# Order of the products, the forget rows, the early up pairs and the last statistics of a decoder layer on one core

## The chip, the core and the metric

The kernel runs on one core of a Trainium2 chip. The metric is the device time of one execution in microseconds (us), the median of the runs. Below, PE is TensorE (PEld its weight loads), DVE is VectorE, ACT is ScalarE, POOL is GpSimd and SP is SyncE, which issues the DMAs.

## The reference

One decoder layer on 1024 positions of width 1024, in fp32. What matters here:

```python
# z = h @ W_in: gates, queries, keys, values and the forget rows of the recurrence
f = lb + (1.0 - lb) * jax.nn.sigmoid(f_logit)
log_f = jnp.log(f); k = 1.0 - f
b = jnp.cumsum(gc, axis=3)               # gc: log_f in chunks of 64 positions
q_in = qc * jnp.exp(b); k_in = kc * jnp.exp(-b); k_out = kc * jnp.exp(b_last - b)
# three mixers: the recurrence, window attention, attention into a memory; gated sum; then
h = layer_norm(alpha * h + mix, g1, b1)
h = layer_norm(alpha * h + relu(h @ W_up)**2 @ W_down, g2, b2)
```

## The kernel before

**Products.** Every 32-bit factor is split into a high and a low part (`split`, lines 76 and 77: ACT casts the high part, then DVE or POOL subtracts to get the low one). The large products are done two row blocks at a time, a *pair*, with seven smaller products in place of eight, numbered 1 to 7 in the code. A product (`prod`, line 61) of a pair in the first projection is twelve 128x512 matmuls into one PSUM tile. PSUM tiles have three names: `pz`, `ps` and `pt`. The right factors are sums of row blocks of W, formed on POOL (`prepare`, line 347, tiles R, then W). The left factors `xs[1]` to `xs[7]` are sums of blocks of x: X for products 1 and 2, T for 4, O for 3 and 5, MG for 6, BT for 7. `x_rest` (four calls, k = 0 to 3) forms T, O, MG and BT.

**Begun pairs.** Products 1 and 2 need only X, so the first twelve pairs are begun early: `two` does products 1 and 2, keeps the first result in DRAM (`d_g`) and emits a result block. When `run` later takes up a begun pair, it loads that first result (`p1`) and adds it with DVE (`plus`, through `add` at line 302) to the PSUM tile `pz` after product 6, and again after product 7, which goes on in the same tile. So product 7 may begin only when DVE's add after product 6 has read the tile. Product 3 goes on in product 5's tile `pt` and is put off into the next pair (`late`, `rest`), after DVE has read that tile.

**First projection.** Sixteen pairs: 0 to 3 and 4 to 7 are the gate rows, 8 to 11 the rows `w_hg` with a silu, 12 to 15 the forget rows `w_hf`, which are not begun and have all seven products in a row. `forget` (lines 407 to 423) runs once for each of these four when its 128x2048 result is complete: two affine maps, a logarithm (ACT), four scans of 128x512 (DVE), an exponential and a subtraction, then a store to `d_b`.

**Up projection.** Its first `EARLY` = 10 pairs are begun by `first_two`; between them `flip_h1` transposes row blocks of the normalised activation (lines 908 and 920), which other products' left factors need.

**Tail.** `last_rows` does the last down products in eight bands of 128 rows. For each band the two halves are added from PSUM, mean and variance are formed (bands 2 and 3 with `bn_stats` on DVE, the six others with sums accumulated by ACT at lines 1167 and 1178 and small DVE steps from line 1174 on) and `norm_rows` normalises: small steps, a power on POOL (line 1238), a scaling on ACT (1244), two multiply and add steps on DVE and POOL (1245, 1246), and the store.

The text of the kernel names tiles and engines; the framework under it places each instruction in its engine's order, and the engines run their rows in that order.

Of the kernel before, what the change touches and what calls it, by code (L numbers as in the profile page):

```python
# [15 lines left out]
P = 128  # L16
# [11 lines left out]
NFF = 4096 // 256  # L28
EARLY = 10
EARLY_Z = 12  # L30
# [5 lines left out]
def hybrid_layer(ctx: ExitStack, tc: tile.TileContext, a: dict, out: bass.AP):  # L36
# [321 lines left out]
    def run(ws, p1, held, emit):  # L358
# [40 lines left out]

    zrows = [("w_gate", 0), ("w_gate", 16), ("w_hg", 0), ("w_hf", 0)]  # L400

# [4 lines left out]

    def forget(i, f, ks):
        for b in range(4):
            h = 2 * (i - 12) + b % 2
            nc.scalar.activation(ks[b // 2][:, b % 2], f[:, b, :], AF.Identity, scale=nc1[:, h:h + 1], bias=c1[:, h:h + 1])  # L410
            nc.sync.dma_start(d_z[i, b], ks[b // 2][:, b % 2])
            nc.vector.tensor_scalar(out=f[:, b, :], in0=f[:, b, :], scalar1=c1[:, h:h + 1], scalar2=c1b[:, h:h + 1],
                                    op0=ALU.mult, op1=ALU.add)
# [49 lines left out]
    def z_first(i):  # L463
        def emit(b, o, s_):
            t = st("G", [P, TH])
            add(t, o, s_)
            if i // 4 == 2:
                u = st("G", [P, TH])
                nc.scalar.activation(u, t, AF.Tanh, scale=0.5)
                nc.vector.scalar_tensor_tensor(out=t, in0=u, scalar=1.0, in1=t, op0=ALU.add, op1=ALU.mult)  # L470
# [231 lines left out]
    def hg_gates(b4, hf):  # L702
        fk = st("T", [P, 4, TH])
        gg = st("T", [P, 4, TH])
        for pp in range(2):
            i = 2 * b4 + pp
            nc.sync.dma_start(fk[:, 2 * pp:2 * pp + 2, :], d_z[12 + i, 2 * hf:2 * hf + 2].rearrange("b p t -> p b t"))
            nc.sync.dma_start(gg[:, 2 * pp:2 * pp + 2, :], d_b[i, 2 * hf:2 * hf + 2].rearrange("b p t -> p b t"))
        return fk, gg

    def hg_head(hf, h, fk, gg, x, v, oh, ol):
# [44 lines left out]
        def outp():  # L756
# [8 lines left out]
            box["sg"] = zgate(2, h, hf)  # L765
            ss = small(4)
# [18 lines left out]
    for hf in range(NH):  # L785
# [354 lines left out]
    def last_rows(bs):  # L1140
# [15 lines left out]
        for b in bs:  # L1156
            bn = sb.tile([P, 4, 6], F32, tag="bn", name=nm("bn"), bufs=8)
            own = b in (2, 3)
            ss = small(2)
            parts = []  # L1160
            for ch in range(2):
                v = pa[((2, 3), (4, 5))[b // 4][ch]][:, b % 4, :]
                add(v, v, oo[b, ch])
                if own:
                    nc.vector.bn_stats(out=bn[:, ch, :], in_=v)
                else:
                    nc.scalar.activation(st("G", [P, TH]), v, AF.Copy, accum_out=ss[:, ch:ch + 1])
                parts.append((v, slice(ch * TH, (ch + 1) * TH)))
            mv = small(2)
            if own:  # L1170
                nc.vector.bn_aggr(out=mv, in_=bn[:, 0:2, :])
            else:
                neg, qq = small(1), small(2)
                nc.vector.tensor_tensor(out=mv[:, 0:1], in0=ss[:, 0:1], in1=ss[:, 1:2], op=ALU.add)
                nc.vector.tensor_scalar(out=neg, in0=mv[:, 0:1], scalar1=-1.0 / D, scalar2=None, op0=ALU.mult)
                nc.vector.tensor_scalar(out=mv[:, 0:1], in0=mv[:, 0:1], scalar1=1.0 / D, scalar2=None, op0=ALU.mult)
                for ch in range(2):
                    nc.scalar.activation(st("G", [P, TH]), parts[ch][0], AF.Square, bias=neg, accum_out=qq[:, ch:ch + 1])  # L1178
                nc.vector.tensor_tensor(out=mv[:, 1:2], in0=qq[:, 0:1], in1=qq[:, 1:2], op=ALU.add)
                nc.vector.tensor_scalar(out=mv[:, 1:2], in0=mv[:, 1:2], scalar1=1.0 / D, scalar2=None, op0=ALU.mult)  # L1180
            norm_rows(nc, small, parts, mv, lng, lnb, LN_EPS, mhalf,
# [144 lines left out]
```

## Time and profile before

| | us |
|---|---|
| median of 3 runs (2188.57 to 2189.2) | 2188.59 |
| the profiled execution's own time | 2191.78 |
| its span, first to last instruction | 2189.8 |
| PE busy (94% of the span) | 2068.2 |
| DVE busy (56%) | 1236.1 |
| POOL busy (44%) | 972.7 |
| ACT busy (40%) | 869.0 |

PE's mean granted clock over the span is 0.975 of full speed. The stages stand in this order: from 56 to 135 us the twelve `two` calls, to 327 the begun pairs 0 to 11, to 446 the pairs 12 to 15, then the mixers, the first layer norm, from about 1500 the up and down projections, and from 2161.4, when the last matmul ends, 28.4 us without PE. The table gives shares over all stages; what a stage waits for has to be read inside it.

### The profile page before, as it was taken

Reading aid. Unit: us, or ns where it says so; the run is one execution under the profiler, and the core shown is the slowest. Engines: PE = TensorE matmul, PEld = TensorE weight load, DVE = VectorE, ACT = ScalarE, POOL = GpSimd, SP = SyncE. Lnnn points to the kernel's source line nnn. Section 1 sums busy time; section 2 is a strip of 40 time slices with the busy share of each in tenths; the row PEclk is TensorE's granted clock in tenths of the full one; section 3 lists DMA queues with packets and bytes.
Section 4 is the critical chain, followed back from the end, with each engine's and each line's share of the span. In section 5 each row is a group of like instructions: output and inputs, shape, how many; then the busy total and the mean of one; then the engine's idle time right before and its main releaser. Section 6 shows DMA issues by size and latency. Waiting matters only on the chain. (4 is left out here: it accounts for less than half of the span.)

```text
span 2189.8 us, 27001 instructions
## 1 busy us (share of the span) xinstructions
PE 2068.2 (94%) x10050; PEld 1700.8 (78%) x10050; DVE 1236.1 (56%) x2080; ACT 869.0 (40%) x1550; POOL 972.7 (44%) x477
## 2 busy tenths in 40 slices
PE   8978889899999999999999999999899999999994
PEld 8757767677788899777778889887678887788773
DVE  5552244777624336356753424536566655699896
ACT  5322223554424334325433413333544455533334
POOL 2465555522122432742213242275433345777764
PEclk9989999999999999999999999999999999999997
DMA  8653333351224423544122442354556546655322
GB/s 288 207 164 120 116 123 99 128 183 59 68 87 155 129 85 96 184 140 155 59 68 87 164 127 89 113 183 146 189 191 227 188 142 217 238 174 190 98 67 77
DMA packets 129923, 307.69 MB, mean 141 GB/s; under 512 B 11473, under 2 KB 24961, under 8 KB 129793
## 3 DMA queue, kind: packets, MB, share of 16 engines
q1 hardware_dynamic: 128896, 302.81, 42.1%
q10 hardware_dynamic: 896, 3.16, 0.4%
q8 instruction: 79, 1.29, 0.3%
q14 instruction: 52, 0.42, 0.1%
HBM read 236.71 MB, written 69.22 MB: 140 GB/s over the span
## 5 line engine op out<-in xcount | busy, mean ns | idle before, releaser
L77 POOL TENSOR_TENSOR W<-R,W 128x1024 fp32r<-128x1024 f32 x205 | 501.8, 2448 | 882.2 <-ACT W L76 843.1
L76 ACT CAST W<-R 128x1024 fp32r<-128x1024 f32 (+1 forms) x303 | 303.8, 1003 | 541.7 <-PE pz L61 235.5
L61 PE MATMUL pz<-X,W 128*128 128x512 f32 x2016 | 490.9, 398 | 11.5 <-ACT T L76 7.4
L61 PEld LDWEIGHTS pz<-X,W 128*128 128x128 f32 x2016 | 378.3, 191 | 93.9 <-ACT T L76 8.6
L61 PE MATMUL pz<-O,W 128*128 128x512 f32 x1152 | 267.2, 391 | 0.0
L61 PEld LDWEIGHTS pz<-O,W 128*128 128x128 f32 x1152 | 214.9, 188 | 46.3 <-issue 1.5
L61 PE MATMUL pt<-O,W 128*128 128x512 f32 x768 | 191.4, 402 | 16.0 <-DVE T L302 15.9
L77 DVE TENSOR_TENSOR W<-R,W 128x1024 fp32r<-128x1024 f32 (+1 forms) x100 | 118.9, 1190 | 136.5 <-ACT W L76 136.2
L61 PEld LDWEIGHTS pt<-O,W 128*128 128x128 f32 x768 | 147.4, 194 | 52.6 <-DVE T L302 21.7
L61 PE MATMUL pz<-BT,W 128*128 128x512 f32 x384 | 110.6, 445 | 26.7 <-DVE G L302 26.7
L61 PEld LDWEIGHTS pz<-BT,W 128*128 128x128 f32 x384 | 82.3, 218 | 51.3 <-DVE G L302 27.0
L61 PE MATMUL ps<-W,BT 128*128 128x512 f32 x360 | 98.1, 390 | 5.3 <-DVE X L302 3.3
L61 PE MATMUL ps<-T,W 128*128 128x512 f32 x384 | 95.3, 392 | 7.0 <-POOL W L77 6.6
L77 POOL TENSOR_TENSOR BT<-R,BT 128x1024 fp32r<-128x1024 f32 x27 | 75.5, 2798 | 58.0 <-ACT BT L76 58.0
L61 PE MATMUL pz<-W,BT 128*128 128x512 f32 x354 | 96.3, 390 | 1.4 <-DVE O L302 1.4
L61 PE MATMUL pz<-W,X 128*128 128x256 f32 x768 | 95.8, 284 | 0.0
L61 PE MATMUL ps<-X,W 128*128 128x512 f32 x384 | 93.8, 393 | 0.0
L61 PE MATMUL pz<-MG,W 128*128 128x512 f32 x384 | 93.7, 389 | 0.0
L61 PEld LDWEIGHTS pz<-W,X 128*128 128x128 f32 x768 | 93.1, 192 | 0.0
L61 PEld LDWEIGHTS ps<-T,W 128*128 128x128 f32 x384 | 72.8, 190 | 23.3 <-POOL W L77 7.1
L302 DVE TENSOR_TENSOR T<-pt,G 128x512 f32<-128x512 f32 x64 | 43.9, 686 | 80.7 <-PE pt L61 80.7
L61 PEld LDWEIGHTS ps<-X,W 128*128 128x128 f32 x384 | 73.4, 191 | 16.3 <-DVE G L302 0.6
(286 smaller groups left out, 3453.8 us busy)
## 6 DMA issues: line engine op xcount, KB each, us to landing
R<-d_ff SPq DMA_DIRECT2D x49, 512.0 KB, 3.8
R<-in_w_b_dram SPq DMA_DIRECT2D x48, 512.0 KB, 3.5
R<-in_w_up_dram SPq DMA_DIRECT2D x42, 512.0 KB, 4.1
R<-in_w_gate_dram SPq DMA_DIRECT2D x40, 512.0 KB, 3.7
d_ff<-T SPq DMA_DIRECT2D x56, 256.0 KB, 2.8
G<-d_z SPq DMA_DIRECT2D x48, 256.0 KB, 3.1
d_ff<-S SPq DMA_DIRECT2D x48, 256.0 KB, 2.3
T<-in_w_down_dram SPq DMA_DIRECT2D x12, 1024.0 KB, 5.1
```

The costliest lines, as they stand in the source:

```text
L61: nc.tensor.matmul(o, lhsT=l, rhs=r, start=start, stop=stop, skip_group_check=more)
L76: (hi_copy or nc.scalar.copy)(hi, src)
L77: (lo_eng or nc.gpsimd).tensor_tensor(out=lo, in0=src, in1=f32(hi), op=ALU.subtract)
L302: nc.vector.tensor_tensor(out=o, in0=a_, in1=b_, op=op)
```

## The change

Six things change.

- In `run` of a begun pair the order of the products is 4, 6, 5, 7 in place of 4, 5, 6, 7, so that product 5 stands between DVE's add after product 6 and product 7.
- In `two` the low part of W is subtracted on DVE, not on POOL. All nine steps of each `x_rest` (four combinations and five low parts) are on POOL, where seven were on DVE; the calls follow the begun pairs 1, 3, 6 and 8, not 2, 4, 6 and 8.
- The forget rows become pairs 4 to 7 and are begun; the silu rows become pairs 12 to 15. `forget` handles each 128x512 block by itself and stores it; the new `log_sums` (eight calls, each after one of the pairs 8 to 15) reads half a pair back from `d_b` and does logarithm, two scans, exponential and subtraction there. The indices of `d_z` follow.
- `EARLY` is 12, and the four `flip_h1` calls follow the begun up pairs 2, 4, 6 and 8, not 1, 3, 5 and 7.
- In the tail all eight bands take their statistics with `bn_stats` and `bn_aggr` on DVE; ACT's accumulating passes and the small steps on them go.

```diff
-EARLY = 10
+EARLY = 12
         def part(j, src, e):
-            split(xs[j][0][:, k], xs[j][1][:, k], src, nc.gpsimd if e else nc.vector)
-
-        combine(t[0], t[1], part, nc.vector)
+            split(xs[j][0][:, k], xs[j][1][:, k], src, nc.gpsimd)
+
+        combine(t[0], t[1], part, nc.gpsimd)
...
     def two(src, keep, emit):
-        w1 = halves(load_raw(src), nc.gpsimd)
+        w1 = halves(load_raw(src), nc.vector)
...
         if p1 is not None:
-            c, b_ = four(), five()
+            c = four()
         prod(o, w4, 0, 6, p1 is not None)
         s2 = copy_out(o) if p1 is None else plus(o, p1)
         if p1 is None:
             c = four()
+        else:
+            b_ = five()
         prod(o, w3, 0, 7, False)
...
-    zrows = [("w_gate", 0), ("w_gate", 16), ("w_hg", 0), ("w_hf", 0)]
+    zrows = [("w_gate", 0), ("w_hf", 0), ("w_gate", 16), ("w_hg", 0)]
...
+    def forget(i, b, f):
+        h = 2 * (i - 4) + b % 2
+        k_ = st("G", [P, TH])
+        nc.scalar.activation(k_, f, AF.Identity, scale=nc1[:, h:h + 1], bias=c1[:, h:h + 1])
+        nc.sync.dma_start(d_z[i, b], k_)
+        nc.vector.tensor_scalar(out=f, in0=f, scalar1=c1[:, h:h + 1], scalar2=c1b[:, h:h + 1], op0=ALU.mult,
+                                op1=ALU.add)
+        nc.sync.dma_start(d_b[i - 4, b], f)
+
+    def log_sums(i, half):
+        f = st("S", [P, 2, TH])
+        rows = d_b[i - 4, 2 * half:2 * half + 2].rearrange("b p t -> p b t")
+        nc.sync.dma_start(f, rows)
         nc.scalar.activation(f, f, AF.Ln)
-        for b in range(4):
+        for b in range(2):
             nc.vector.tensor_tensor_scan(out=f[:, b, :], data0=reset, data1=f[:, b, :], initial=0.0,
                                          op0=ALU.mult, op1=ALU.add)
...
+        nc.scalar.activation(elc[:, h:h + 2, half, :], f.rearrange("p h (c t) -> p h c t", t=64)[:, :, :, 63], AF.Exp)
...
-                                in1=gp[:, :, 0, 63:64].broadcast_to([P, 16, 64]), op=ALU.subtract)
-        nc.sync.dma_start(d_b[i - 12].rearrange("b p t -> p b t"), f)
+                                in1=gp[:, :, 0, 63:64].broadcast_to([P, 8, 64]), op=ALU.subtract)
+        nc.sync.dma_start(rows, f)
...
     for i in range(EARLY_Z):
         two(zsrc(i)[0], z_keep(i), z_first(i))
-        if i in (2, 4, 6, 8):
-            x_rest(i // 2 - 1)
+        if i in (1, 3, 6, 8):
+            x_rest((1, 3, 6, 8).index(i))
     for i in range(16):
         ws = prepare(*zsrc(i), i >= EARLY_Z)
         run(ws, z_p1(i)() if i < EARLY_Z else None, None, z_emit(i))
+        if i >= 8:
+            log_sums(4 + (i - 8) // 2, i % 2)
...
     for i in range(EARLY):
         first_two(i)
-        if i % 2 and i < 8:
+        if i in (2, 4, 6, 8):
             deferred.pop(0)()
...
         for b in bs:
-            own = b in (2, 3)
...
                 add(v, v, oo[b, ch])
-                if own:
-                    nc.vector.bn_stats(out=bn[:, ch, :], in_=v)
-                else:
-                    nc.scalar.activation(st("G", [P, TH]), v, AF.Copy, accum_out=ss[:, ch:ch + 1])
+                nc.vector.bn_stats(out=bn[:, ch, :], in_=v)
...
-            if own:
-                nc.vector.bn_aggr(out=mv, in_=bn[:, 0:2, :])
-            else:
-                neg, qq = small(1), small(2)
...
+            nc.vector.bn_aggr(out=mv, in_=bn[:, 0:2, :])
```

What stands in the engines' rows, first PE in the begun pair 1 of the first projection, before: the end of product 6 (MG), four matmuls of the next pair's product 4 (ps, T) and the start of product 7 (BT).

```order
L61 MATMUL pz_1289<-MG_117,W_1280 128x512 x2
L61 MATMUL pz_1289<-MG_118,W_1280 128x512
L61 MATMUL pz_1289<-MG_117,W_1280 128x512
L61 MATMUL ps_1401<-T_121,W_1372 128x512
L61 MATMUL ps_1401<-T_122,W_1372 128x512
L61 MATMUL ps_1401<-T_121,W_1372 128x512 x2
L61 MATMUL pz_1289<-BT_119,W_1284 128x512
L61 MATMUL pz_1289<-BT_120,W_1284 128x512
```

The same place of the changed kernel, where `pt` with O is product 5 of the same pair:

```order
L61 MATMUL pz_1297<-MG_117,W_1288 128x512 x2
L61 MATMUL pz_1297<-MG_118,W_1288 128x512
L61 MATMUL pz_1297<-MG_117,W_1288 128x512
L61 MATMUL pt_1340<-O_116,W_1284 128x512 x12
L61 MATMUL pz_1297<-BT_119,W_1292 128x512
L61 MATMUL pz_1297<-BT_120,W_1292 128x512
```

Between products 6 and 7 stand twelve matmuls in place of four.

Second, POOL while the begun pairs of the first projection are started, before: the low parts of W alternate with two of the nine steps of each `x_rest` (S is the loaded part of x).

```order
L77 TENSOR_TENSOR W_825<-R_823,W_825 128x1024
L77 TENSOR_TENSOR O_116<-S_767,O_116 128x512
L77 TENSOR_TENSOR W_881<-R_879,W_881 128x1024
L77 TENSOR_TENSOR T_122<-S_767,T_121 128x512
L77 TENSOR_TENSOR W_919<-R_917,W_919 128x1024
```

The same stretch of POOL in the changed kernel:

```order
L77 TENSOR_TENSOR W_604<-R_602,W_604 128x1024
L202 TENSOR_TENSOR S_729<-S_731,S_729 128x512
L204 TENSOR_TENSOR S_731<-S_731 128x512
L77 TENSOR_TENSOR O_115<-S_731,O_115 128x512
L77 TENSOR_TENSOR O_116<-S_729,O_116 128x512
L77 TENSOR_TENSOR BT_120<-S_731,BT_119 128x512
L206 TENSOR_TENSOR S_731<-S_731,S_729 128x512
L208 TENSOR_TENSOR S_729<-S_729,S_731 128x512
L77 TENSOR_TENSOR MG_118<-S_731,MG_117 128x512
L77 TENSOR_TENSOR T_122<-S_729,T_121 128x512
```

All nine steps of an `x_rest` stand in a row on POOL, and the low parts of W have gone from it.

Third, DVE where the forget rows' sums are formed, before (pair 13; T_2558 is the 128x2048 result, L416 the four scans, L302 the adds that read PSUM):

```order
L302 TENSOR_TENSOR T_2703<-ps_2690,G_2652 128x512
L321 COPY G_2718<-pz_2639 128x512
L416 SCALAR_TENSOR_TENSOR T_2558<-reset,T_2558 128x512 x4
L422 TENSOR_TENSOR T_2558<-T_2558 128x16x64
L321 COPY G_2745<-pz_2639 128x512
L412 TENSOR_SCALAR T_2703<-T_2703,c_76,c1b 128x512
```

In the changed kernel, in the begun pairs around pair 8 (S is the part read back, L424 the scans, L429 the subtraction, the adds from pz those after products 6 and 7):

```order
L424 SCALAR_TENSOR_TENSOR S_2302<-reset,S_2302 128x512
L302 TENSOR_TENSOR G_1950<-pz_1905,G_1903 128x512
L414 TENSOR_SCALAR T_1871<-T_1871,c_76,c1b 128x512
L77 TENSOR_TENSOR W_2004<-R_1996,W_2004 128x512
L424 SCALAR_TENSOR_TENSOR S_2302<-reset,S_2302 128x512
L424 SCALAR_TENSOR_TENSOR S_2406<-reset,S_2406 128x512
L429 TENSOR_TENSOR S_2302<-S_2302 128x8x64
L302 TENSOR_TENSOR G_1977<-pz_1905,G_1903 128x512
L424 SCALAR_TENSOR_TENSOR S_2406<-reset,S_2406 128x512
L302 TENSOR_TENSOR T_1979<-ps_1925,G_1977 128x512
L302 TENSOR_TENSOR T_1979<-pt_1952,G_1977 128x512
```

The scans stand one or two at a time between the adds of begun pairs, in place of four in a row among the copies of a pair with seven products.

## Rows read from the trace of the kernel before

**Rows 1.** Page, part 1: busy time, share of the span and instructions of each engine.

```profile
PE 2068.2 (94%) x10050; PEld 1700.8 (78%) x10050; DVE 1236.1 (56%) x2080; ACT 869.0 (40%) x1550; POOL 972.7 (44%) x477
```

**Rows 2.** Waits of PE, whole span: us in total, times, longest.

```profile
PE pz L61 <- DVE G L302: 26.7, 13, 3.3
PE pt L61 <- DVE T L302: 15.9, 5, 4.3
PE pt L920 <- DVE R L208: 11.2, 3, 5.7
...
PE pz L61 <- ACT T L76: 7.4, 3, 2.6
```

**Rows 3.** Stretches: length, engines' busy us (instructions), then PEclk, DMA share, GB/s.

```profile
207.23:222.99 15.76, 13.90 (x61) 11.19 (x61) 4.49 (x6) 4.48 (x6) 9.92 (x7) 1.00 0.40 134
222.99:240.38 17.39, 15.53 (x60) 12.35 (x61) 4.49 (x6) 4.48 (x6) 9.92 (x7) 0.90 0.38 122
...
345.00:466.00 121.00, 104.43 (x424) 83.93 (x423) 81.87 (x84) 63.58 (x75) 61.19 (x29) 0.93 0.43 140
1500.00:1605.00 105.00, 88.91 (x379) 72.14 (x377) 67.25 (x96) 49.75 (x79) 51.02 (x28) 0.93 0.53 175
```

**Rows 4.** Timeline of PE, pairs 0 and 1: start, us, operation, idle before.

```profile
135.16 2.99 PE L61 MATMUL ps<-T,W 128*128 128x512 f32 x12 [0.37 <-DVE G L302]
...
150.67 1.22 PE L61 MATMUL ps<-T,W 128*128 128x512 f32 x2 [6.63 <-POOL W L77]
154.51 5.29 PE L61 MATMUL pz<-BT,W 128*128 128x512 f32 x12 [2.62 <-DVE G L302]
```

**Rows 5.** Groups by line, 56 to 161.6 us: busy, mean ns, idle before.

```profile
L206 DVE TENSOR_TENSOR S<-S,S 128x512 f32<-128x512 f32 x4 | 9.0, 2245 | 0.1
...
L77 POOL TENSOR_TENSOR O<-S,O 128x512 fp32r<-128x512 f32 x4 | 5.5, 1376 | 21.2 <-ACT O L76 21.2
...
L202 DVE TENSOR_TENSOR S<-S,S 128x512 f32<-128x512 f32 x4 | 2.8, 694 | 24.8 <-DMA S<-in_xT_dram 24.8
```

**Rows 6.** Timeline of POOL, first step of the first `x_rest`.

```profile
70.94 1.61 POOL L77 TENSOR_TENSOR O<-S,O 128x512 fp32r<-128x512 f32 x1 [5.60 <-ACT O L76]
```

**Rows 7.** DMA issues, 56 to 330 us: KB each, median us to landing.

```profile
S<-in_xT_dram SPq DMA_DIRECT2D x7, 512.0 KB, 5.6
```

**Rows 8.** Timeline of all engines, begun pair 5, between products 6 and 7.

```profile
239.65 0.68 DVE L302 TENSOR_TENSOR G<-pz,G 128x512 f32<-128x512 f32 x1
...
240.38 0.96 PE L61 MATMUL pz<-BT,W 128*128 128x512 f32 x3 [1.86 <-DVE G L302]
```

**Rows 9.** Groups by line and shape, 161 to 466 us.

```profile
L416 DVE TENSOR_TENSOR_SCAN T<-reset,T 128x512 f32<-128x512 f32 x16 | 29.9, 1928 | 4.4 <-ACT T L414 4.4
...
L414 ACT ACT_TABLE_LOAD x4 | 5.1, 1283 | 0.1
```

**Rows 10.** Timeline of PE, pairs 12 to 15.

```profile
351.55 5.49 PE L61 MATMUL pt<-O,W 128*128 128x512 f32 x12 [4.32 <-DVE T L302]
...
431.69 2.88 PE L61 MATMUL ps<-T,W 128*128 128x512 f32 x12
434.41 2.88 PE L61 MATMUL pz<-BT,W 128*128 128x512 f32 x12
```

**Rows 11.** Timeline of PE, two of the four flips of the up stage.

```profile
1527.93 0.88 PE L920 MATMUL pt<-cst,T 128*128 128x128 f32 x4 [4.66 <-DVE R L208]
...
1560.05 1.09 PE L920 MATMUL pt<-cst,T 128*128 128x128 f32 x4 [5.74 <-DVE R L208]
```

**Rows 12.** Timeline of ACT in the tail: the scaling of two bands.

```profile
2142.57 0.82 ACT L1244 ACTIVATE X<-X,sm,sm 128x512 f32<-128x512 f32 x1 [1.52 <-DVE sm L1242]
...
2150.33 0.82 ACT L1244 ACTIVATE X<-X,sm,sm 128x512 f32<-128x512 f32 x1 [1.99 <-DVE sm L1242]
```

**Rows 13.** Timeline of PE, its last matmuls.

```profile
2160.59 0.84 PE L61 MATMUL pz<-W,MG 128*128 128x512 f32 x3
```

**Rows 14.** Groups of DVE by line, 2128 us to the end.

```profile
L1165 DVE BATCH_NORM_STATS2 bn<-X 128x6 f32<-128x512 f32 x2 | 1.4, 688 | 0.0
```

More of the change, by code (lines that the diff above doesn't have):

```diff
@@ L405, in zsrc @@
         return a[name][m], a[name][m + 1]
-    def forget(i, f, ks):
-        for b in range(4):
[L409 to L413, printed above, removed]
+    def forget(i, b, f):
[10 more added lines that the diff above has]
+        nc.sync.dma_start(f, rows)
         nc.scalar.activation(f, f, AF.Ln)
-        for b in range(4):
+        for b in range(2):
             nc.vector.tensor_tensor_scan(out=f[:, b, :], data0=reset, data1=f[:, b, :], initial=0.0,
                                          op0=ALU.mult, op1=ALU.add)
-        h = 2 * (i - 12)
-        nc.scalar.activation(elc[:, h:h + 2, :, :].rearrange("p h f c -> p f h c"),
-                             f.rearrange("p (f h) (c t) -> p f h c t", f=2, t=64)[:, :, :, :, 63], AF.Exp)
+        h = 2 * (i - 4)
+        nc.scalar.activation(elc[:, h:h + 2, half, :], f.rearrange("p h (c t) -> p h c t", t=64)[:, :, :, 63], AF.Exp)
         gp = f.rearrange("p h (c u t) -> p (h c) u t", u=2, t=64)
         nc.vector.tensor_tensor(out=gp[:, :, 0, :], in0=gp[:, :, 0, :],
-                                in1=gp[:, :, 0, 63:64].broadcast_to([P, 16, 64]), op=ALU.subtract)
-        nc.sync.dma_start(d_b[i - 12].rearrange("b p t -> p b t"), f)
+                                in1=gp[:, :, 0, 63:64].broadcast_to([P, 8, 64]), op=ALU.subtract)
+        nc.sync.dma_start(rows, f)
     def z_emit(i):
@@ L433, in emit @@
             add(f, o, s_)
-            if i // 4 != 2:
+            if i // 4 != 3:
                 nc.scalar.activation(f, f, AF.Tanh, scale=0.5)
@@ L439, in emit @@
                 nc.vector.scalar_tensor_tensor(out=f, in0=th, scalar=1.0, in1=f, op0=ALU.add, op1=ALU.mult)
-            if i < 12:
+            if i // 4 == 1:
+                forget(i, b, f)
+            else:
                 nc.sync.dma_start(d_z[i, b], f)
-            elif b == 2:
-                forget(i, box[0], [st("S", [P, 2, TH]) for _ in range(2)])
         return emit
@@ L466, in emit @@
             add(t, o, s_)
[L467 to L470, printed above, removed]
-            else:
-                nc.scalar.activation(t, t, AF.Tanh, scale=0.5)
-            nc.sync.dma_start(d_z[i, b], t)
+            nc.scalar.activation(t, t, AF.Tanh, scale=0.5)
+            if i // 4 == 1:
+                forget(i, b, t)
+            else:
+                nc.sync.dma_start(d_z[i, b], t)
         return emit
@@ L706, in hg_gates @@
             i = 2 * b4 + pp
-            nc.sync.dma_start(fk[:, 2 * pp:2 * pp + 2, :], d_z[12 + i, 2 * hf:2 * hf + 2].rearrange("b p t -> p b t"))
+            nc.sync.dma_start(fk[:, 2 * pp:2 * pp + 2, :], d_z[4 + i, 2 * hf:2 * hf + 2].rearrange("b p t -> p b t"))
             nc.sync.dma_start(gg[:, 2 * pp:2 * pp + 2, :], d_b[i, 2 * hf:2 * hf + 2].rearrange("b p t -> p b t"))
@@ L764, in outp @@
                 mm(oo[:, cs], qm[:, cs], sp[:, n, :], False, n == 3)
-            box["sg"] = zgate(2, h, hf)
+            box["sg"] = zgate(3, h, hf)
             ss = small(4)
@@ L828, in hybrid_layer @@
         for m in range(8):
-            proj("w_b2", m, (oh, ol), merged, zgate(1, m, hf))
+            proj("w_b2", m, (oh, ol), merged, zgate(2, m, hf))
         oh = st("O", [P, NK, TH], F32R)
@@ L1157, in last_rows @@
             bn = sb.tile([P, 4, 6], F32, tag="bn", name=nm("bn"), bufs=8)
-            own = b in (2, 3)
-            ss = small(2)
             parts = []
@@ L1163, in last_rows @@
                 add(v, v, oo[b, ch])
-                if own:
-                    nc.vector.bn_stats(out=bn[:, ch, :], in_=v)
-                else:
-                    nc.scalar.activation(st("G", [P, TH]), v, AF.Copy, accum_out=ss[:, ch:ch + 1])
+                nc.vector.bn_stats(out=bn[:, ch, :], in_=v)
                 parts.append((v, slice(ch * TH, (ch + 1) * TH)))
             mv = small(2)
-            if own:
-                nc.vector.bn_aggr(out=mv, in_=bn[:, 0:2, :])
-            else:
-                neg, qq = small(1), small(2)
[L1174 to L1180, printed above, removed]
+            nc.vector.bn_aggr(out=mv, in_=bn[:, 0:2, :])
             norm_rows(nc, small, parts, mv, lng, lnb, LN_EPS, mhalf,
```

## The prediction

> **What bounds the kernel.** I read the page first: PE is busy for 2068 of 2189.8 us [rows 1], so nothing but PE's own work, its clock and its gaps is to be had, about 120 us of gaps with the head and the tail. PE's waits come next [rows 2]. Four rows say where the change can gain: 26.7 us in 13 waits of `pz` for an add at L302 (the `plus` after product 6), 15.9 us in 5 waits of `pt` for an add into T (product 3 waiting in the last four pairs), 11.2 us at the flips, and 7.4 us for x_rest's stretch at the start. Then the stretches, because a gap also costs clock [rows 3]: two begun pairs with the same instructions take 15.76 us at a granted clock of 1.00 and 17.39 us at 0.90. The second holds 3.4 us at half clock (1.2 against 2.4 GHz), so one such window costs 1.63 us, 0.48 of its length. A gap of 1.9 us is followed by such a window in eight of the ten pairs 1 to 10 counted below.
>
> **The products' order.** Ten begun pairs after 161.6 us wait for `plus` between 6 and 7. The row shows it: DVE's add starts at 239.65, PE's product 7 stands until 240.38 after 1.86 us idle [rows 8]. The ten sum to 19.2 us (the 26.7 less 2.6 at 154.51 and 4.9 in the up stage). In the new order twelve matmuls stand in the gap, and twelve matmuls at full clock take 434.41 − 431.69 = 2.72 us [rows 10]. The wait to be covered is 1.86 us with a few matmuls of the next product in front of it already; from the end of product 6 the add needs its 0.7 us and a start, some 2.8 us with those four matmuls counted, of which 2.72 are now covered. So the 19.2 go, and with them eight windows of 1.63, 13.0. **Gain 32.** What must be ready instead is POOL: 9.92 us busy per pair [rows 3], and a load and waits between, so I estimate a POOL period of about 14 us against PE's 5 x 2.72 = 13.6. That is tight, and it is the first rival.
>
> **The start.** Before, product 4 of pair 0 starts at 135.16, after three waits in the twelve `two` calls, and then 6.63 and 2.62 us are lost in pair 1 [rows 4]. Afterwards DVE no longer holds x_rest, its copies from PSUM come at once, and the twelve `two` end about 13 us earlier (7.4 of waits, the rest clock). But product 4 needs all of x_rest, and that is now one chain on POOL: 36 steps of 1.376 [rows 5] are 49.5 us, from about 70 [rows 6], with three reloads of 5.6 us [rows 7] that cannot overlap since the S buffers are only freed by the last step, 16.8, and some 6.7 of pair 0's own sums standing in between. That gives 143 us: product 4 starts 8 us later than 135.16. The 9.25 us of gaps behind it are then mostly gone, since DVE and POOL's loads have had time. **Gain 1**, from −14 to +6. The lower end is from the shared path of DVE and POOL: two DVE steps of the same shape took 694 ns (L202) and 2245 ns (L206) [rows 5], the second while POOL was at work. If DVE's twelve low parts at about 1.2 us each (the L77 kind) hold POOL off, that is 14.3 us more on the chain.
>
> The Trainium skill, page "SBUF — State Buffer", section "SBUF: two separate sides", says that VectorE with two SBUF inputs and GpSimd take a shared port pair as an exclusive lock for a whole instruction, and the other blocks. The pair of 694 and 2245 ns agrees with it. By that rule alone the start would be a loss of 14 and not a gain of 1, which is one of the rivals below, since x_rest and the low parts of W both have two SBUF inputs and now sit on these two engines.
>
> **Forget rows.** They are begun pairs now and their scans are spread over pairs 8 to 15. The waits in the last four pairs came from four scans in a row: 4 x 1.93 [rows 9] stand ahead of the adds that product 3 waits for, 4.32 us for the first [rows 10], 15.2 in four. With two scans and 0.75 us of subtraction per pair, at most 4.6 us, in a pair of seven products (19 us), I expect no wait left. PEclk of 0.93 over 121 us [rows 3] is about 17 us at half clock, 8 us of loss. 15.2 + 8 less 1 for leftovers: **gain 22.** The silu steps that move there take 1.3 us of DVE each, four a pair, and fit.
>
> The price is paid in the pairs 5 to 11. DVE gets scans ahead of adds that PE waits for. The slack there is small: after product 7 three adds of 0.69 (2.06 us) must end before product 3 starts, and eleven matmuls of product 4 (2.5 us) cover them: 0.4 us. The order shows where scans stand: between the two adds of a pair with W's low part 1.2, two scans 3.9 and a subtraction, 6.6 us against two products, 5.4, and once one scan more before the next adds. That makes about 0.7 us late in three places and 2.7 in one, 4.8; two or three half-clock windows of 1.63 and some wait for ACT's logarithms and table loads (1283 ns [rows 9], about six more of them), 2 us, make 10 to 11. **Loss 10**, from 3 to 40.
>
> **The up stage.** The three flips that wait 11.2 [rows 2, 11] and two waits of 3.3 and 1.6 sum to 16.1; PEclk 0.93 over 105 us is 14.7 us at half clock, 7.0. One `two` (5.4 us) more before each flip should cover the first (4.66 us) and not all of the third: I leave 7.5 us of waits and half of the clock. 23.1 − 11 = 12, less 2 for the two more begun pairs' DVE and DRAM work: **gain 10**, from 3 to 18.
>
> **The tail.** PE ends at 2161.4 [rows 13], the span at 2189.8: 28.4 us. ACT scales one band 7.76 us after the other [rows 12], while PE makes a band in 24 matmuls, 5.4 us: the statistics went to and fro between ACT and DVE. With `bn_stats` (0.688 [rows 14]) DVE needs per band two adds 1.36, two statistics 1.38, aggregation and small steps 1.1, two multiplications 1.4, about 5.2, plus a wait for POOL's power and slower steps beside POOL: 5.6 to 6.2. So DVE ends one to five us behind PE, and a last band's chain is about 11.5 (adds and statistics 2.8, small steps and power 1.8, scaling and the two products and adds 3.6, issue and landing 3). 28.4 − 11.5 − 5: **gain 12**, from 5 to 17.
>
> **Sum.** 1 + 32 − 10 + 22 + 10 + 12 = 67 us off 2189.8, span 2122.8; own time 2191.78 − 67 = 2124.8. The profiled execution is 3.2 above the median, so the forecast is 2121.6, said as 2122. Nothing in the stages between 470 and 1500 us moves on PE.
>
> **Rivals.** (1) *POOL's period bounds the begun pairs.* Then a pair takes the 15.76 us of the undisturbed pair and not 13.9, and the ten lose 10 x 1.9 = 19: 2141. For it: 9.92 us of work with a load and two hand-overs; against it: POOL waits for others in every pair of before. (2) *The scans and logarithms hold up the adds in all eight calls.* Two scans less 0.4 slack, 3.4, with a window of 1.63: 5 x 8 = 40 in place of 10: 2152. For it: 0.4 us of slack; against: in the row shown only one place has three scans. (3) *The shared port lengthens x_rest's chain*: −14 in place of +1: 2137. (4) *The gaps go and the half-clock windows stay*, since a gap shorter than 1.86 can still be followed by one: 13 + 8 + 5 = 26 lost: 2148. Against it: the 15.76 pair had a 1.86 gap too, and full clock. (5) *Slower*: the read-back of `log_sums`. Logarithm, scans and subtraction stand in ACT's and DVE's rows ahead of tanh, W's casts and the adds. If a load that follows its store by little sits at the head, each of the eight calls stops PE for the whole chain: load 3.1, logarithm 1.0, two table loads 2.6, scans 3.9, subtraction 0.75, 11.3 us, 90 in all. In place of the 10, that turns +67 to −13: 2202. It decides from (67 + 10) / 8 = 9.6 us per call. (6) *The change doesn't do what it says*: the framework's order puts things back; but the rows of PE show product 5 between 6 and 7, so that is open only for waits, and then 2185 to 2190.
>
> **Numbers.** Forecast (2108 to 2136) 0.50; rival 1 0.16; rival 2 0.15; rival 3 0.08; rival 4 0.05; rival 5 0.04; rival 6 0.02. The range goes from 2100, the forecast with the up and tail terms at their upper ends, to 2158, which holds rival 2 with some spread; outside stay rivals 5 and 6 and the ends. 0.2% is 4.4 us, about what a measurement of this kernel tells from no change: faster 0.94, same 0.02, slower 0.04.
>
> **What the profile would show.** Right: the waits of `pz` for DVE G at L302 down from 26.7 to a few, a begun pair near 14 us at a clock near 1.00, no `pt` wait for T of over 1 us in pairs 12 to 15, product 4 of pair 0 near 143 behind one long wait for POOL, flips waiting under 6 us together, and a tail of some 16 us. Wrong: waits of `ps` or `pt` for POOL W in each begun pair (rival 1), for DVE adds behind L424 (rival 2), product 4 of pair 0 past 155 (rival 3), clock 0.9 in pairs without gaps (rival 4), PE idle over 9 us at each log_sums (rival 5).

## The result: faster by 0.7%, a fifth of the forecast

The changed kernel takes 2173.92 us (2168.97 to 2175.96) against 2188.58, a ratio of 0.993 with an interval of 0.9911 to 0.995: 15 us off, where 67 were forecast and 2122 was said. 2174 lies above the range of 2100 to 2158. (The time of the kernel before moved between 2188.6 and 2192.4 us from one group of runs to the next, so kernels are compared below by their ratios to it, 0.1% being 2.2 us.)

The profile after, first the page's busy times, as [rows 1]:

```profile
PE 2054.4 (94%) x10050; PEld 1690.3 (78%) x10050; DVE 1229.5 (57%) x2060; ACT 859.2 (40%) x1512; POOL 974.0 (45%) x493
```

The waits of PE over the whole span, as [rows 2] (us, times, longest):

```profile
PE pt L61 <- DVE T L302: 28.0, 11, 6.8
PE pz L61 <- DVE G L302: 22.6, 7, 7.8
PE pt L927 <- DVE R L208: 9.5, 3, 3.9
PE ps L61 <- POOL W L77: 8.0, 2, 6.2
```

The waits of `pz` for the add fell in number from 13 to 7 and hardly in time, and the waits of `pt` for an add into T grew from 15.9 to 28.0 us: the wait has changed its place. Both kernels issue the same 10050 matmuls, so the start of the same matmul, by its number, can be compared from stage to stage. The begun pairs are counted off in 60 matmuls each from the start of product 4 of pair 0, the pairs 12 to 15 in 84. The up stage starts at matmul 7306; the row for it takes the matmuls 7400 to 8000, where its waits lie.

| stage | before, us | after, us | gained | forecast |
|---|---|---|---|---|
| to product 4 of pair 0 | 135.16 | 132.12 | 3.0 | |
| pair 0 | 26.30 | 32.94 | −6.6 | 1 (both) |
| pairs 1 to 5 | 85.23 | 77.19 | 8.0 | 32 less 10 |
| pairs 6 to 11 | 99.71 | 115.35 | −15.6 | (both) |
| pairs 12 to 15 | 99.70 | 78.21 | 21.5 | 22 |
| mixers, layer norm, to matmul 7400 | 1074.3 | 1072.1 | 2.2 | 0 |
| matmuls 7400 to 8000 (up stage) | 157.95 | 161.60 | −3.7 | 10 |
| to the last matmul | 482.7 | 484.6 | −1.9 | 0 |
| after it | 28.4 | 19.6 | 8.8 | 12 |

The row of pairs 12 to 15 looks as forecast, the tail's is smaller, the gain of the begun pairs 1 to 5 is used up by the pairs 6 to 11, and the up stage has the other sign. The two rows from pair 6 to 15 need care: with the new order a wait changes sides between them. Product 3 of pair 11 waits 4.32 us at 351.55 before [rows 10], within the row of pairs 12 to 15; after the change it still waits, but just ahead of that row:

```profile
357.60 4.60 PE L61 MATMUL pt<-O,W 128*128 128x512 f32 x12 [3.98 <-DVE T L302]
```

Cut on either side of this product, at the matmuls 1334 and 1406, pairs 1 to 10 lose 2.6 us (171.1 to 173.7), what lies between takes 23.0 and 23.3, and the rest to pair 15 gains 16.8 (90.5 to 73.8). The stretches of the changed kernel (columns as [rows 3]): pair 3, pair 6, pairs 7 to 11, pairs 12 to 15.

```profile
195.77:211.22 15.45, 13.90 (x62) 11.18 (x61) 4.50 (x6) 4.49 (x7) 9.90 (x7) 1.00 0.45 138
...
242.25:267.01 24.76, 16.96 (x61) 13.16 (x60) 18.76 (x18) 13.15 (x18) 12.67 (x7) 0.79 0.58 196
267.01:357.60 90.59, 73.52 (x302) 58.54 (x300) 50.70 (x55) 46.88 (x59) 50.64 (x28) 0.94 0.60 199
357.60:435.80 78.20, 78.20 (x336) 64.18 (x337) 43.59 (x49) 25.45 (x34) 47.15 (x24) 0.98 0.42 133
```

Pair 3 runs at full clock and still takes 15.45 us, as long as the pair of [rows 3] with full clock and a gap. In pair 6 DVE is busy for 18.76 of 24.76 us. From 357.60 on, pairs 12 to 15 have PE busy all the time.

### The profile page after: what moved, and what is told of

Its sections match the earlier page's. It is cut to its first block, busy times and chain, and to the rows that moved or that the text cites. A ratio compares the mean times of both kernels' runs of the same rounds, so it can differ in the third digit from the quotient of the medians.

```text
span 2174.1 us, 27034 instructions
## 1 busy us (share of the span) xinstructions
PE 2054.4 (94%) x10050; PEld 1690.3 (78%) x10050; DVE 1229.5 (57%) x2060; ACT 859.2 (40%) x1512; POOL 974.0 (45%) x493
## 4 chain that ended last, share of the span: by engine, by line
PE 64%; POOL 10%; DVE 9%; issue 5%; DMA 3%; ACT 3%; SPq 0%; POOLq 0%; ACTq 0%; DVEq 0%
PE pz L61 41%; PE ps L61 14%; PE pt L61 8%; POOL W L77 4%; POOL R L347 2%; DVE O L302 1%; DVE X L302 1%; DMA R<-in_w_up_dram 1%; DVE T L302 1%; DVE W L77 1%; ACT W L76 1%; POOL MG L77 1%; DMA R<-in_w_hf_dram 1%; PE pt L545 1%; DMA R<-in_w_gate_dram 1%
## 5 line engine op out<-in xcount | busy, mean ns | idle before, releaser
L77 POOL TENSOR_TENSOR W<-R,W 128x1024 fp32r<-128x1024 f32 x193 | 469.0, 2430 | 871.3 <-ACT W L76 808.8
L77 DVE TENSOR_TENSOR W<-R,W 128x1024 fp32r<-128x1024 f32 (+1 forms) x112 | 140.1, 1252 | 165.7 <-ACT W L76 164.2
L61 PE MATMUL pt<-O,W 128*128 128x512 f32 x768 | 196.2, 406 | 28.1 <-DVE T L302 28.0
L61 PE MATMUL pz<-BT,W 128*128 128x512 f32 x384 | 97.3, 404 | 22.6 <-DVE G L302 22.6
L61 PEld LDWEIGHTS pz<-BT,W 128*128 128x128 f32 x384 | 74.3, 195 | 41.2 <-ACT W L76 9.6
L61 PE MATMUL ps<-T,W 128*128 128x512 f32 x384 | 95.9, 395 | 7.9 <-POOL W L77 6.2
L347 POOL TENSOR_TENSOR R<-R,R 128x512 f32<-128x512 f32 x48 | 67.0, 1396 | 48.1 <-DMA R<-in_w_gate_dram 28.2
L302 DVE TENSOR_TENSOR T<-pt,G 128x512 f32<-128x512 f32 x64 | 43.9, 686 | 77.1 <-PE pt L61 77.1
```

What stands on the lines that cost most here:

```text
L61: nc.tensor.matmul(o, lhsT=l, rhs=r, start=start, stop=stop, skip_group_check=more)
L77: (lo_eng or nc.gpsimd).tensor_tensor(out=lo, in0=src, in1=f32(hi), op=ALU.subtract)
L302: nc.vector.tensor_tensor(out=o, in0=a_, in1=b_, op=op)
L347: nc.gpsimd.tensor_tensor(out=o, in0=a_, in1=b_, op=op)
```

## What sets a begun pair: POOL's cycle

One begun pair of the changed kernel, all engines (timeline, start and us):

```profile
185.16 1.29 POOL L347 TENSOR_TENSOR R<-R,R 128x512 f32<-128x512 f32 x1 [4.05 <-DMA R<-in_w_hf_dram]
...
190.25 2.66 POOL L347 TENSOR_TENSOR R<-R,R 128x512 f32<-128x512 f32 x2
...
191.57 0.62 ACT L76 CAST W<-R 128x512 fp32r<-128x512 f32 x1 [6.77 <-POOL R L347]
192.22 1.24 DVE L77 TENSOR_TENSOR W<-R,W 128x512 fp32r<-128x512 f32 x1 [5.41 <-ACT W L76]
...
193.38 0.68 DVE L302 TENSOR_TENSOR G<-pz,G 128x512 f32<-128x512 f32 x1
193.52 3.28 SPq L311 DMA_DIRECT2D R<-in_w_hf_dram  x2
194.07 2.37 POOL L77 TENSOR_TENSOR W<-R,W 128x1024 fp32r<-128x1024 f32 x1 [1.16 <-ACT W L76]
...
194.70 0.68 DVE L302 TENSOR_TENSOR T<-pt,G 128x512 f32<-128x512 f32 x1
...
195.44 3.01 PE L61 MATMUL pt<-O,W 128*128 128x512 f32 x12 [1.42 <-DVE T L302]
...
200.60 1.29 POOL L347 TENSOR_TENSOR R<-R,R 128x512 f32<-128x512 f32 x1 [4.16 <-DMA R<-in_w_hf_dram]
```

Read it backwards. PE's product 3 waits for the add into T; that add and the two ahead of it stand in DVE's row behind the low part of W at 192.22, which waited 5.41 us for ACT's cast, which waited for POOL's difference. And POOL begins a pair late because it waits for the load of R, 4.05 us here and 4.16 in the next pair: the two loads go out one by one from 193.52, when DVE's low part of W (to 193.46) and then POOL's (to 196.44) have read the old R tiles. POOL's round, 9.90 us of work, 1.16 of waiting for ACT's cast and 4.16 for the load, is 200.60 − 185.16 = 15.44 us. That it is as long as the pair proves nothing by itself, since everything repeats once a pair; but no wait in it is for PE, so PE can't shorten it. Before the change the same low part of W stood ahead of the add after product 6, just before the row at 239.65 in [rows 8]:

```profile
232.94 1.05 ACT L76 CAST W<-R 128x1024 fp32r<-128x1024 f32 x1 [2.81 <-PE pt L61]
...
234.07 2.40 POOL L77 TENSOR_TENSOR W<-R,W 128x1024 fp32r<-128x1024 f32 x1 [2.38 <-ACT W L76]
...
237.86 0.62 ACT L76 CAST W<-R 128x512 fp32r<-128x512 f32 x1 [3.34 <-POOL R L347]
...
238.51 1.22 DVE L77 TENSOR_TENSOR W<-R,W 128x512 fp32r<-128x512 f32 x1 [4.92 <-ACT W L76]
```

So the gap of 1.86 us wasn't the add's latency; it was POOL's lateness, handed on by DVE's row. Before, the round did run through PE as well: POOL's low part waited 2.38 us for ACT's cast, and that for PE's product 3 in `pt`.

Three kernels test it. The new order alone (edit: product 5 after the add, as in the diff), expected:

> Before with the new order of products 4, 6, 5, 7 alone. Theory P (each begun pair is set by POOL's cycle, some 11.3 us of work and 4.1 us of waiting for R): the wait of pz for the add after product 6 goes, a wait of pt for the add into T of 1.4 to 1.6 us comes in its place, a pair stays at 15.4 to 15.8 us, and only the half-clock windows go: 10 to 15 us off, about 2175. Rival G (the gap was the add's latency): no new wait, a pair at 13.9 us, 30 off, about 2158.

Measured 2164.47, ratio 0.9883 (0.987 to 0.9897), 25.6 us off: more than the whole change gives. Its pairs (windows):

```profile
199.43:214.70 15.27, 13.90 (x61) 11.19 (x60) 4.50 (x6) 4.48 (x7) 9.86 (x7) 1.00 0.41 138
214.70:229.66 14.96, 13.89 (x61) 11.18 (x60) 4.51 (x6) 4.49 (x7) 9.88 (x7) 1.00 0.43 140
```

The new wait of `pt` is there (26.6 us in 13 waits over the whole span), most pairs take 15.0 to 15.5 us and not 13.9, and in the pairs 1 to 10 the half-clock windows are gone. The saving is above theory P's 10 to 15: in the profile pair 0 and pair 1 also gained 4.0 and 3.4 us, and most pairs ran below 15.4; the pairs 1 to 10 together gained 21.7 (171.1 to 149.5). Next, POOL is relieved and the order of products left as before, `add` being DVE's:

```diff
-        sub(r1[:, H], r1[:, H], r0[:, L])
+        add(r1[:, H], r1[:, H], r0[:, L], ALU.subtract)
...
-        sub(r0[:, H], r0[:, H], r1[:, H])
+        add(r0[:, H], r0[:, H], r1[:, H], ALU.subtract)
```

> Before with the same two differences on DVE, in the old order of products. Theory P: product 6's add no longer stands behind a low part of W that waits for POOL, so the gap of 1.86 us and the half-clock windows mostly go without any new order: 20 to 30 us off, about 2165. Rival G (the gap is the add's own latency behind only four matmuls): the gap stays near 1.9 us and the time within 5 us of before.

2168.19, ratio 0.9898 (0.9886 to 0.9911): 22 us off with the old order of products. A pair takes 14.74 us, and PE's gap before product 7 is 0.85 us:

```profile
228.67 0.68 DVE L302 TENSOR_TENSOR G<-pz,G 128x512 f32<-128x512 f32 x1
...
229.41 3.01 PE L61 MATMUL pz<-BT,W 128*128 128x512 f32 x12 [0.85 <-DVE G L302]
```

That decides against rival G: the gap shrinks when POOL is early, with the same four matmuls in it. Both together:

> Before with the new order of products, and with the third and fourth difference of prepare on DVE, not POOL (2.65 us of POOL's work a pair, 1.4 us of DVE's). Theory P (POOL's cycle, 11 us of work and 4 of waiting for R, sets a pair): the cycle falls to about 13, a pair to PE's 13.6 to 13.9, ten pairs save about 1.3 each against the order alone (2164.5): about 2151. Rival W (the new wait of pt comes from DVE's own row, the low part of W ahead of the add, whatever POOL does): no gain or a loss, 2164 to 2170.

2160.37, ratio 0.9866 (0.9853 to 0.9878), 29 us off and not the 39 of theory P: the time lies between the two theories, and its interval overlaps that of the order alone. In the profiles the pairs 1 to 11 take 160.0 us against 167.5, as P has it but by half, and the start with pair 0 takes 4.0 more. POOL's work is now 7.34 us of a pair, and the pair 14.3:

```profile
201.83:216.20 14.37, 13.89 (x62) 11.18 (x60) 5.26 (x8) 4.49 (x7) 7.34 (x4) 1.00 0.45 153
216.20:230.44 14.24, 13.86 (x61) 11.19 (x60) 5.26 (x8) 4.47 (x7) 7.33 (x4) 1.00 0.44 147
```

The round through R is still there: POOL's first steps of two pairs start at 189.02 and 203.41, 14.39 apart, with 3.77 us of waiting for the load and 3.18 for ACT's cast.

## The forget rows among begun pairs

The part alone (rows as begun pairs 4 to 7, sums after pairs 8 to 15):

> Before with the forget rows as begun pairs 4 to 7 and the sums of half a pair after pairs 8 to 15 alone. Theory: the scans and the logarithm's wait for ACT cost 14 to 20 us in pairs 6 to 12, pairs 12 to 15 save 20 to 22 against before: within 5 us of before, 2183 to 2190. Rival (the prediction's terms): 22 less 10, 12 off, 2176.

2182.44, ratio 0.9965 (0.9951 to 0.9978), 7.6 us off, between the two. Pairs 12 to 15 take 84.4 us against 99.7, pairs 6 to 11 110.0 against 99.7. In the changed kernel pair 6 shows what happens:

```profile
240.57 1.06 ACT L422 ACTIVATE S<-S 128x1024 f32<-128x1024 f32 x1
...
241.67 4.44 DVE L424 TENSOR_TENSOR_SCAN S<-reset,S 128x512 f32<-128x512 f32 x2 [1.14 <-ACT S L422]
...
246.03 0.66 DVE L302 TENSOR_TENSOR G<-pz,G 128x512 f32<-128x512 f32 x1
246.18 1.28 ACT L427 ACT_TABLE_LOAD   x1 [3.61 <-DVE S L424]
...
247.74 0.69 DVE L429 TENSOR_TENSOR S<-S 128x512 f32<-128x512 f32 x1 [1.05 <-ACT elc L427]
248.35 0.68 DVE L302 TENSOR_TENSOR T<-ps,G 128x512 f32<-128x512 f32 x1
...
249.68 1.65 PE L61 MATMUL pt<-O,W 128*128 128x512 f32 x3 [6.82 <-DVE T L302]
```

DVE's row has two scans, an add that PE waits for, the subtraction, which waits for ACT's table load and exponential, and then the adds; PE stands for 6.82 us. Scans or ACT? The changed kernel without the scans (the running sums are missing), and without the logarithm and the exponential (a scaling in their place, the exponential an identity):

```diff
-        for b in range(2):
-            nc.vector.tensor_tensor_scan(out=f[:, b, :], data0=reset, ...)
...
-        nc.scalar.activation(f, f, AF.Ln)
+        nc.scalar.activation(f, f, AF.Identity, scale=-0.02)
```

> The changed kernel without the sixteen scans of log_sums (the running sums are left out; the logarithms, the last positions' exponential and the subtraction stay). Theory S (DVE's scans, 1.93 us each, stand in DVE's row ahead of the adds of begun pairs): pairs 6 to 11 fall from 115 to near 100 us, 10 to 16 off the changed kernel, 2158 to 2164. Rival T (ACT's logarithm, exponential and table loads, for which DVE's row waits, are the cause): under 5 off.

> The changed kernel with the logarithm and the exponential of log_sums replaced by a scaling, so that ACT loads no tables there (the sums are of other numbers; the scans stay). Theory S: under 6 off the changed kernel. Rival T: 10 to 16 off, 2158 to 2164.

Without scans 0.9873 (0.9859 to 0.9886), 12.5 us less than the changed kernel's 0.993 by the ratios (7 to 18 by their intervals) and 9.2 by the two profiled executions; without table loads 0.9932, no change. Pairs 6 to 11 with the scans and without:

```profile
242.25:357.60 115.35, 90.49 (x362) 71.70 (x360) 69.46 (x73) 60.04 (x76) 63.31 (x35) 0.91 0.60 199
239.04:345.76 106.72, 88.50 (x362) 70.62 (x360) 43.39 (x56) 60.08 (x76) 60.55 (x35) 0.93 0.64 216
```

DVE's busy time falls by 26 us and the stretch by 8.6, to 106.72 and not to theory S's 100; with the new order alone it takes 92.94. So the scans are shown to cost some 9 us there, and the table loads by themselves nothing; what the other 14 us are is not shown. In pair 6 itself the scans are worth only 1.1 us: without them it takes 23.65, since its subtraction waits for ACT all the same:

```profile
239.87 1.28 ACT L424 ACT_TABLE_LOAD   x1
...
241.42 1.39 DVE L426 TENSOR_TENSOR S<-S 128x512 f32<-128x512 f32 x1 [3.01 <-ACT elc L424]
...
244.07 2.50 PE L61 MATMUL pt<-O,W 128*128 128x512 f32 x5 [4.64 <-DVE T L302]
```

Scans and ACT's chain stand one behind the other in DVE's row, so with one gone the other remains; a kernel without both, and one without the maps of `forget`, were not run. A run that missed its aim: all eight `log_sums` after pairs 12 to 15 in the text.

```diff
-        if i >= 8:
-            log_sums(4 + (i - 8) // 2, i % 2)
+        if i >= 12:
+            for half in range(2):
+                log_sums(i - 8, half)
```

> The changed kernel with all eight log_sums after the pairs 12 to 15 (two each), not after 8 to 15. Theory S (the waits of 2 to 7 us in pairs 6 to 12 are scans and ACT's logarithms in the rows ahead of the adds): pairs 6 to 11 go back to 15.4 us each, 12 to 15 stay near 19 to 20, the waits of pt for T from 250 to 360 us go: 12 to 18 off the changed kernel, 2156 to 2162. Rival M (the forget maps and their stores of pairs 4 to 7, or the reordered loads, hold the pairs up): less than 4 off.

2170.63, ratio 0.9915 (0.9901 to 0.993), not clear of the changed kernel. All sixteen scans stand at the same places of DVE's row in both kernels (the 119th, 120th, 125th and 126th of its 2060 instructions, and on), so moving the call moved none of them, and this run tells nothing about theory S or M. The places themselves matter: in the changed kernel the scans start between 241.7 and 332.2 us, from the end of pair 5 to pair 10. The calls in the text follow the pairs 8 to 15, but no scan stands beside the pairs 12 to 15.

## The other parts

x_rest on POOL and W's low parts on DVE, alone, and the changed kernel without this part:

> Before with x_rest on POOL, the low parts of W in two on DVE and the calls after pairs 1, 3, 6, 8 alone. Theory: the chain on POOL ends near 143 us, the first add of p1 waits for its load late, and pair 1 begins 3 to 4 us later than before (161.45): 2188 to 2193. Rival (the prediction's term): 1 us off, 2187 to 2188.

> The changed kernel with x_rest and the low parts of W in two as before (DVE and POOL, after pairs 2, 4, 6, 8). Theory: pair 0 takes 22.3 us as with the order alone and not 32.9, so about 10 us off the changed kernel, 2164. Rival: the part costs alone 6.5 us and no more here: 2167 to 2168; or nothing, if the time comes back in the forget pairs: 2174.

Alone 2196.81, ratio 1.0029 (1.0019 to 1.004), 6 us slower; taking it out gives 2165.4, 0.9886 (0.9871 to 0.9901), 9.6 us better than with it. The part costs time, and more in company. In the changed kernel (all engines):

```profile
136.69 2.33 POOL L77 TENSOR_TENSOR W<-R,W 128x1024 fp32r<-128x1024 f32 x1
...
139.07 3.78 PE L61 MATMUL ps<-T,W 128*128 128x512 f32 x8 [6.22 <-POOL W L77]
...
141.06 1.10 DVE L77 TENSOR_TENSOR W<-R,W 128x512 fp32r<-128x512 f32 x1 [9.83 <-ACT W L76]
...
142.09 0.68 DVE L321 COPY G<-pz 128x512 f32<-128x512 f32 x1
...
150.44 0.38 SPq L465 DMA_DIRECT2D G<-d_g  x1
...
155.84 0.69 DVE L302 TENSOR_TENSOR G<-pz,G 128x512 f32<-128x512 f32 x1 [5.42 <-DMA G<-d_g]
...
156.59 3.72 PE L61 MATMUL pz<-BT,W 128*128 128x512 f32 x8 [7.06 <-DVE G L302]
```

POOL's chain ends where the prediction put it, with T at 143.3; two of pair 0's own steps, at 136.69 and 139.10, stand among the last nine. But a low part of W of pair 0 waits 9.83 us in DVE's row for ACT's cast, which waits for POOL, and behind it stand the copies of the last begun pairs; the load of pair 0's first result goes out at 150.44, after their stores in SP's row, and the add after product 6 waits for it. In company much of the loss is here: the same wait is 7.06 us, and 1.50 in the changed kernel without this part. It isn't this part's alone, as with the new order alone it is 5.76. With the part alone, in the old order, what is new is a wait of 3.18 us for POOL's W within product 4 of pair 0.

The up stage with both edits, and the flips' alone:

> Before with twelve begun up pairs and the flips one turn later alone. Theory: the first flips wait 1 to 3 us less, and the first two pairs of the up stage wait longer for the first result's load and for DVE, 7.8 us at the first product 7: within 5 us of before, 2186 to 2193. Rival (the prediction's term): 10 us off, 2180.

> Before with the flips after the up pairs 2, 4, 6, 8 alone, ten begun up pairs. Theory: the flips' waits fall from 11.2 to about 9.5 and the loss of 7 us at the first product 7 is from the last flip's turn standing closer to the first loads, or from twelve begun pairs; if it is the flips, 2188 to 2195 as with both; if it is the twelve begun pairs, 2184 to 2188.

Both 2195.1, ratio 1.002 (1.0011 to 1.0028), 4 us slower; the flips alone 2185.64, 0.9976 (0.9967 to 0.9984), 5 us faster. So the flips' turns gain and the two more begun pairs cost some 10. The profiles place less than that in the up stage, 2.7 us of gain (178.3 to 175.7 for matmuls 7306 to 8000) and 4.6 of cost (to 180.3); where the rest lies is not shown. The waits for the flips, 11.2 us before, are 9.7 with both edits and 9.0 with the turns alone. With both edits pair 0 of the up stage waits 6.90 us before product 7, and DVE's row shows what is ahead of the add:

```profile
1585.45 0.69 DVE L302 TENSOR_TENSOR R<-R,R 128x512 f32<-128x512 f32 x1 [1.90 <-DMA R<-in_w_up_dram]
...
1586.66 2.62 DVE L302 TENSOR_TENSOR R<-R 128x512 f32<-128x512 f32 x1
1589.20 1.41 DVE L302 TENSOR_TENSOR R<-R,R 128x512 f32<-128x512 f32 x2
1590.52 0.69 DVE L302 TENSOR_TENSOR G<-pz,G 128x512 f32<-128x512 f32 x1
```

The sums of W for this pair come late and stand before it, as in the first projection. Why they come later with twelve begun pairs than with ten was not taken apart. The tail:

> Before with the tail's statistics on DVE alone. Theory: the time from the last matmul to the end falls from 28.4 to about 20 us as in the changed kernel, 8 to 9 us off, 2180. Rival: part of that comes from other parts of the change, then under 4 us off.

2183.83, ratio 0.9967 (0.9954 to 0.9979), 7 us off: this part is worth the same alone and in company (8.8 us in the profile).

Then versions put together: the new order, the two differences on DVE and the tail; the same with the forget rows begun; the same with the forget rows in pairs 12 to 15 as before, but summed by halves; and this with the flips' turns. The edit of the third and fourth, against the changed kernel:

```diff
-    zrows = [("w_gate", 0), ("w_hf", 0), ("w_gate", 16), ("w_hg", 0)]
+    zrows = [("w_gate", 0), ("w_gate", 16), ("w_hg", 0), ("w_hf", 0)]
...
+        if i >= 13:
+            for hv in range(2):
+                log_sums(i - 1, hv)
```

> Before with the new order of products, two differences of prepare on DVE, and the tail's statistics on DVE. The parts are in different stages and should add: 30 and 7 off, 2153.

> The same with the forget rows as begun pairs 4 to 7 and their sums after pairs 12 to 15 (two each). Theory S: pairs 12 to 15 fall from 92.8 us to near 78, a few us go back in pairs 4 to 7 (forget's maps): 8 to 14 off the version without it, 2139 to 2146. Rival M: no gain, 2150 to 2156.

> Order of products, two differences on DVE, the tail's statistics on DVE (2150.6), and the forget rows in pairs 12 to 15 as before, but mapped block by block and summed by halves, two scans at a time. Theory S: no scans among begun pairs, the waits of 3.2 to 4.3 us in pairs 12 to 15 and their half-clock windows go: 10 to 18 off 2150.6, 2133 to 2141. Rival M (the maps and the read-back keep the pairs up): 2148 to 2155.

> The same with the flips after the up pairs 2, 4, 6, 8 and ten begun pairs, which alone took 4 to 5 us off: 3 to 5 less than the version without it.

| version | us | ratio (interval) |
|---|---|---|
| order, differences, tail | 2150.64 | 0.982 (0.9806 to 0.9833) |
| with forget rows begun | 2159.97 | 0.9864 (0.985 to 0.9877) |
| with sums by halves in pairs 12 to 15 | 2146.77 | 0.9792 (0.9779 to 0.9805) |
| and the flips' turns | 2144.06 | 0.9782 (0.9768 to 0.9795) |

The first adds up as expected. On it the begun forget rows cost 9.6 us where alone they gained 7.6. In the first version pairs 6 to 11 take 88.6 us with DVE busy for 42.6, in the second 110.4 with 68.6:

```profile
230.28:318.89 88.61, 83.14 (x362) 66.99 (x360) 42.59 (x57) 26.28 (x37) 41.84 (x22) 1.00 0.41 136
```

```profile
228.89:339.28 110.39, 90.13 (x361) 71.13 (x359) 68.61 (x84) 59.37 (x75) 42.31 (x23) 0.93 0.59 199
```

With the forget rows' steps among them the pairs 6 to 10 take 95.9 us with the old order (`p_forget`) and 92.1 here, without them 85.9 and 71.6: most of what the order and the differences had gained there is lost. The second version's scans stand in begun pairs too (from 225.6 us on), wherever its call is, so its expectation fell with `lateC`'s. The third gained 6 us of 10 to 18: three of four waits of 3.2 to 3.8 us in pairs 12 to 15 stayed (3.25, 3.38, 3.25 and 1.32). The fourth, 48 us off, beats both kernels; its step of 2 us on the third lies inside the intervals.

## Why the prediction was wrong, step by step

- **The products' order, 32 forecast.** The step that failed is the reading of [rows 8]: the 1.86 us were priced as the time of the add and its cover, and what held the add's start at 239.65 was not looked up. It was a low part of W behind ACT's cast behind POOL. The prediction had the right suspect, POOL's period, with an estimate of 14 us and called tight, and gave it 0.16; it is 15.44, since the wait for R of about 4 us lies on it whole. Rival 1's price, a pair of 15.76 us, would have been near: pairs 1 to 5 take 15.4 each and gained 1.6 each, mostly the half-clock windows. Its sign was looked for in the wrong place: in the pairs 1 to 5 no wait of `ps` or `pt` for POOL's W came, but one of `pt` for DVE's add, which stands in its row behind POOL's lateness. Alone the order gave 25.6 us, and in the profile 21.7 in the ten pairs 1 to 10 that the 32 were for.
- **The clock.** Right in part: the half-clock windows went, in pairs 1 to 4, but beside gaps of 1.4 to 1.6 us that stayed. In pairs 6 to 11 they came back with longer waits (granted clock 0.91). Rival 4, windows without gaps, is out.
- **The start, 1 forecast.** POOL's chain ended at 143 as worked out. The term left out what stands behind the late rows on DVE and SP: −3.6 in the sum of both lines, 6 to 10 us by the runs. DVE's copies did not come at once either: three of the `two` calls wait 1.89, 2.21 and 1.61 us for such a copy (L321), and the twelve end 4 us earlier, not 13. A POOL step beside one of DVE's low parts does take longer:

```profile
72.68 1.95 DVE L77 TENSOR_TENSOR W<-R,W 128x1024 fp32r<-128x1024 f32 x1 [5.11 <-ACT W L76]
...
73.49 2.29 POOL L77 TENSOR_TENSOR BT<-S,BT 128x512 fp32r<-128x512 f32 x1
```

  Of the 36 steps four took 2.26 to 2.29 us in this way and one 1.72, the others 1.30 on average: 4.3 us more on the chain, not the 14.3 of rival 3. That 143 came out all the same was luck: each step had been set at 1.376 us. The Trainium skill ("SBUF — State Buffer", section "SBUF: two separate sides") says that of VectorE with two SBUF inputs and GpSimd the one that starts first keeps the shared ports for its whole instruction while the other blocks. The trace agrees: DVE's step ends at 74.63 and POOL's, begun at 73.49, 1.15 us after that.
- **The forget rows' price, 10 forecast.** Right mechanism, wrong size: pairs 6 to 11 take 115.35 us, 22.4 more than with the new order alone. The scans account for some 9 of that; the subtraction's wait for ACT's exponential was not counted, and the rest is not shown. That the order's rows were summed as if each pair began with DVE's row empty, while lateness carries over, is argued and was not tested.
- **Pairs 12 to 15, 22 forecast.** The row's 21.5 agrees by luck: 16.8 are gained, and the rest is the wait that changed sides. Of the four waits of before, three went; the first, 4.32 us, was read as four scans, but its add stood behind POOL too, and it is 3.98 now. Before, just ahead of it:

```profile
348.37 1.21 DVE L77 TENSOR_TENSOR W<-R,W 128x512 fp32r<-128x512 f32 x1 [6.73 <-ACT W L76]
```

  Two scans a pair were to hide in the pairs 12 to 15, and none stand there.
- **The up stage, 10 forecast.** Wrong sign: the flips' turns gave 5, and the price of two more begun pairs, set at 2, is about 10. The waits for the flips and the two others, to fall from 16.1 us to 7.5, are 18.7.
- **The tail, 12 forecast.** Right mechanism, 8.8 in size. DVE starts the last band's first add 4.8 us behind PE's end (2159.29 against 2154.51), within the 5 allowed; from there to the end it takes 14.8 us, not 11.5, as steps of the band before stand in between.

The parts don't add up: alone, the five edits sum to 30 us off (25.6 + 7.6 + 7 − 6 − 4), and together they give 15. What comes off in company is the start's part (9.6 in place of 6) and the forget rows, which alone gain 7.6 and beside the new order and the two differences cost 9.6. The sum of terms had no place for that.

The forecast of faster held, by 0.7%. Rivals 5 and 6 did not occur: the longest wait of PE in pairs 6 to 11 is 6.8 us. The range's lower end was mis-added: the forecast with the up and tail terms at their upper ends is 2109, not 2100.

## What to carry to other kernels

A gap behind an add is priced only after asking what stood ahead of that add in its engine's row, and following that back until a load or a full buffer ends the chain; if that round is as long as the period and doesn't run through the gap's own engine, covering the gap moves the wait and saves little more than the clock. Work put into an engine's idle time is paid for by whoever queues behind it: the forget rows' steps, which cost three waits of 3.2 to 3.8 us among pairs with seven products, lost more than that among begun pairs shortened by the new order. Parts of a change should be timed alone: here one part alone was worth more than all of them together.

## What the runs showed of the hardware that was not expected

Gaps of 1.4 to 1.6 us in every pair, 15.4 us apart, left the granted clock at 1.00 (the pairs at 195.77 and 211.22 us), where gaps of 1.86 us before the change were followed by 3.4 us at half clock in eight of ten pairs and by full clock in the other two.
